# A state-space layer whose block-Toeplitz matrices are built by GpSimd's copies inside SBUF

## The chip, the core and the metric

The kernel runs on one core of a Trainium2 chip. The core has five engines that each work through their own queue of instructions in order: TensorE (PE in the profile), VectorE (DVE), ScalarE (ACT), GpSimd (POOL) and SyncE (SP). SP does nothing but start transfers. The engines wait for one another through semaphores. The metric is the device time of one execution in microseconds (us), as the median of several runs.

## The reference

One decoder layer on a sequence of 512 positions and 1024 channels, all in 32-bit floats. A normalized input `h` goes through one wide projection. Its columns feed a state-space branch (called S5), a dilated attention branch, and gates. Both branches are projected, gated, summed, projected once more and added to the input.

```
proj = h @ w_in                       -> u_s, z_s, q, k, v, z_a, r_s, r_a
S5:   h_t = A h_(t-1) + B u_t         (complex diagonal A; 64 groups, 64 states each, 16 channels each)
      y_t = Re(C h_t) + D u_t
      g   = gelu(y);  y_s = g * sigmoid(g @ w_glu);  y_s = (y_s * silu(z_s)) @ w_ssm_out
attention: 3 head groups, windows (128,1), (512,4), (2048,16), merged by softmax denominators
x + (sigmoid(r_s) * y_s + sigmoid(r_a) * y_a) @ w_o
```

The change touches the computation of `y` and of `gelu(y)`. The gelu is the tanh form, y/2 (1 + tanh(0.798 (y + 0.044715 y^3))).

## The kernel before, in words

**Projections.** Each weight tile of 128 columns is loaded by SP (`w_raw`, 512 KB), split into a high and a low part (`w_hi` on ACT, L93; `w_lo` on DVE, L95), and multiplied in three products for each of 8 row blocks: 24 matmuls of 128x512, which write a PSUM tile `pj` (L108 to L110). There are 3 such PSUM tiles, so the fourth projection from now needs the first one's tile read out by ACT. Projections that depend on nothing but `h` are used as fillers: they keep PE busy while other engines prepare the state-space branch. The last ten of them, `rs` and `ra`, are read out by a tanh on ACT (`th`, L477 and L485) and stored to HBM (`gd`, `rad`).

**The state-space branch** treats the sequence as 64 chunks of 8 positions. Its 64 groups are worked in 8 units of 8 groups, j = 0 to 7. A scan on DVE turns the inputs into the state at the end of every chunk (`Xs`). Then, for each unit:

- `ca_unit(j)` loads C (`cn`), has POOL swap its halves (L681, L682), transposes it on PE (`cps`, L685), and builds on DVE the coefficients `ab` (C times powers of A, L260 to L262). It also loads the D row (`dg`) and has POOL spread it on a diagonal (L697).
- `m_unit(j)` multiplies coefficients by B on PE (`kps`, L706), which gives the 8 impulse-response blocks K_0 to K_7 of each group. Four ACT copies bring them to the tile `kt` of 16 partitions (L710), POOL adds the D diagonal (L711). From `kt` the block-Toeplitz matrix M has to be formed: 128 partitions, where partition block t (16 partitions) holds, for each of 8 groups, the blocks shifted by t, and zeros behind them. The kernel before does it through HBM: SP stores `kt` in a buffer `kd` whose rows of 240 elements end in 112 zeros (L712), waits until it has landed, and loads M back with a source pattern of overlapping rows (L715), into one of three old buffers of the tile `dd`. The zeros are written once for all units, earlier, from a tile `zer` (L672, L673).
- `s_unit(j)` makes the shifted states for the unit, `Ss`, in the tile `uss`: POOL clears the first column of each group (L722), and ACT copies the states one column to the right, as eight copies, four large (L728) and four small (L729), because the states lie in another order than the columns.
- `y_unit(j)` computes y on PE, 32 matmuls with M and 32 with `ab` and `Ss` (`yps`, L739 and L741), read out by ACT (`ysb`, L743).
- `g_unit(j)` transposes y on PE (`yT`, L749) and applies the gelu: copy (L754) and square (L756) on ACT, a scale and add (L757) and a product (L758) on DVE, tanh on ACT (L759), a product on DVE (L760), and the split into `gT_hi` (ACT, L93) and `gT_lo` (DVE, L97).

In the written program unit j's `y_unit` stands together with `m_unit(j + 2)`, `ca_unit(j + 3)`, `s_unit(j + 1)`, `g_unit(j - 1)` and one filler. What follows the branch is the product of `gT` with `w_glu` (`pj` from `gT`), which needs all eight units of `gT` and then keeps PE busy.

**What sets the order.** The order written in Python isn't the order on the engines. A scheduler orders the instructions of each engine by a simulated time line when the program is built, and dependences become semaphore waits. So a changed edit moves instructions on every engine. Memory is shared by tags: `kt` has two buffers, so `kt` of unit j + 2 may be written only when all readers of `kt` of unit j are done; M has three; `Ss` has two.

Of the kernel before, what the change touches and what calls it, by code (L numbers as in the profile page):

```python
# [11 lines left out]
F32 = mybir.dt.float32  # L12
F32R = mybir.dt.float32r
I32 = mybir.dt.int32
AF = mybir.ActivationFunctionType
ALU = mybir.AluOpType
# [4 lines left out]
P = 128  # L21
# [6 lines left out]
Q = 16  # L28
T = 8
C = S // T  # L30
NJ = 8
NI = C // NJ
# [20 lines left out]
def tile_hybrid_block(ctx: ExitStack, tc: tile.TileContext, x, positions, norm_w, w_in, lam_re, lam_im,  # L53
# [3 lines left out]
    pe, act, dve, pool, sp = nc.tensor, nc.scalar, nc.vector, nc.gpsimd, nc.sync  # L57
# [4 lines left out]
    big = ctx.enter_context(tc.tile_pool(name="big", bufs=1))  # L62
    tmp = ctx.enter_context(tc.tile_pool(name="tmp", bufs=6))
    sml = ctx.enter_context(tc.tile_pool(name="sml", bufs=2))
    dram = ctx.enter_context(tc.tile_pool(name="dram", bufs=1, space=DRAM))
# [148 lines left out]
    for h in range(2):  # L214
# [10 lines left out]
        for q in range(KT // 2):  # L225
# [6 lines left out]
            for k in range(2):  # L232
                kk, t = 2 * q + k, slice(256 * h, 256 * h + 256)
# [3 lines left out]
                                         op0=ALU.mult, op1=ALU.subtract)  # L237
# [6 lines left out]
    Xsv = Xs.rearrange("p a i (g j) -> p a g j i", j=NJ)  # L244

    def load_u(j, Uj=None):
        if Uj is None:
            Uj = t2k("Uj")
        sp.dma_start(Uj, ud[j].rearrange("q g s c -> s q g c"))
        return Uj.rearrange("p (g c) -> p g c", g=8)  # L250
# [45 lines left out]
    for h in range(2):  # L296
        for (hi, lo), ps in first:
            for k in range(KT):
                t = slice(256 * h, 256 * h + 256)
# [77 lines left out]
    for n in (1, 2, 4):  # L377
# [3 lines left out]
        a = pw[:, :, 0:n, :]  # L381
# [285 lines left out]

    gT_hi = big.tile([P, KT, S], F32R, name="gT_hi", tag="s3")
    gT_lo = big.tile([P, KT, S], F32R, name="gT_lo", tag="s4")
    kd = dram.tile([8, Q, 8, 240], F32, name="kd")  # L670
    zer = big.tile([P, 8, 112], F32, name="zer", tag="s7b")
    pool.memset(zer, 0.0)  # L672
    sp.dma_start(kd[:, :, :, 128:240].rearrange("j q g k -> (j q) g k"), zer)  # L673

    def ca_unit(j):

# [23 lines left out]
    def m_unit(j, ca, dg):  # L700

        kt = big.tile([Q, 8, T, Q], F32, name="kt", tag=("s7a", "s7b")[j % 2])
        ps = bank("kps")
        for gg in range(8):
            a, b = gg % 4, gg // 4
            pe.matmul(ps[32 * a:32 * a + Q, b * P:(b + 1) * P], BB[:, 8 * j + gg, :], ca[:, gg, 1:9, :],  # L706
                      start=True, stop=True, skip_group_check=True, tile_position=(0, 32 * a))
        kv = kt.rearrange("q (b a) k p -> q a b (k p)", a=4)
        for a in range(4):
            act.copy(kv[:, a], ps[32 * a:32 * a + Q, 0:2 * P].rearrange("q (b m) -> q b m", b=2))  # L710
        pool.tensor_tensor(kt[:, :, T - 1, :], kt[:, :, T - 1, :], dg, op=ALU.add)  # L711
        sp.dma_start(kd[j, :, :, 0:128], kt.rearrange("q g k p -> q g (k p)"))  # L712
        M = (D1, D2, BB2)[j % 3].rearrange("p g q -> p (g q)")
        kj = kd[j]
        sp.dma_start(M.rearrange("p (g k) -> p g k", g=8),  # L715
                     bass.AP(tensor=kj.tensor, offset=kj.offset, ap=[[Q, T], [8 * 240, Q], [240, 8], [1, P]]))
        M = M.rearrange("p (g k) -> p g k", g=8)
        return M

    def s_unit(j):  # L720
        Ss = uss[:, 2 + j % 2].rearrange("p (g c) -> p g c", g=8)
        pool.memset(Ss[:, :, 0:1], 0.0)  # L722
        Sv = Ss.rearrange("p (g two) (j i) -> p two g j i", two=2, j=NJ)
        for h in range(2):
            for a in range(2):
                o = Sv[64 * a:64 * a + 64, h]
                x_ = Xsv[64 * h:64 * h + 64, a, 4 * j:4 * j + 4]
                act.copy(o[:, :, :, 1:NI], x_[:, :, :, 0:NI - 1])  # L728
                act.copy(o[:, :, 1:NJ, 0], x_[:, :, 0:NJ - 1, NI - 1])  # L729
        return Ss  # L730

    def y_unit(j, ca, M, Uj, Ss):
        ysb = t2k("ysb").rearrange("c (t m) -> c t m", t=4)
# [12 lines left out]
    def g_unit(j, ysb):  # L746
        yT = bank("yT")
        for r in range(NB):
            pe.transpose(yT[:, r * P:(r + 1) * P], ysb[:, NB - 1 - r], ident)  # L749

        yv = yT.rearrange("p (r h c) -> p r c h", h=2, r=4)
        s = t2k("gs")
        sv = s.rearrange("p (r c h) -> p r c h", r=4, h=2)
        act.copy(sv, yv)  # L754
        q = t2k("gq")
        act.activation(q, s, AF.Square)  # L756
        dve.tensor_scalar(q, q, 0.044715, 1.0, op0=ALU.mult, op1=ALU.add)  # L757
        dve.tensor_tensor(q, q, s, op=ALU.mult)  # L758
        act.activation(q, q, AF.Tanh, scale=GELU_C)  # L759
        dve.scalar_tensor_tensor(q, q, 1.0, s, op0=ALU.add, op1=ALU.mult)  # L760
        split(gT_hi[:, j], gT_lo[:, j], q, scale=0.5)
# [9 lines left out]
        for f in scan_work[i * len(scan_work) // n_scan:(i + 1) * len(scan_work) // n_scan]:  # L771
            f()

    uss = big.tile([P, 4, 512], F32, name="uss", tag="s6b")
    for j in range(2):
        Us[j] = load_u(j, uss[:, j % 2])
    Ss_[0] = s_unit(0)
    for j in range(8):
        if j + 2 < 8:
            Ms[j + 2] = m_unit(j + 2, cas[j + 2], dgs[j + 2])  # L780
        filler()
        ysbs[j] = y_unit(j, cas.pop(j), Ms.pop(j), Us.pop(j), Ss_.pop(j))
        if j + 3 < 8:
            cas[j + 3], dgs[j + 3] = ca_unit(j + 3)
        if j + 2 < 8:
            Us[j + 2] = load_u(j + 2, uss[:, j % 2])
        if j + 1 < 8:
            Ss_[j + 1] = s_unit(j + 1)
        if j > 0:
            g_unit(j - 1, ysbs.pop(j - 1))  # L790
# [363 lines left out]
```

## Time and profile before

| | |
|---|---|
| median of 3 runs | 746.56 us (746.32 to 746.74) |
| the profiled execution | 746.7 us, of which 744.9 us between first and last instruction |
| PE busy | 695.5 us (93%), 4357 matmuls |
| DVE busy | 463.3 us (62%), 914 instructions |
| ACT busy | 338.0 us (45%), 662 instructions |
| POOL busy | 170.8 us (23%), 304 instructions; it issues no transfers |
| mean granted TensorE clock | 0.975 |
| moved by DMA | 85.41 MB, 115 GB/s |

The profile counts an engine as busy while an instruction runs; issuing a transfer isn't counted. In rows of the time line the first number is the start, the second the duration, both in us, and what stands in brackets is the idle time before it and what ended it. Successive ACT, DVE and PE instructions overlap by some tens of nanoseconds to some hundreds, so a row's start-to-start distance can be less than its duration. "SPq" is the time SP takes to issue a transfer, not the transfer itself. In the text, `yps 3` is unit 3's `yps`, and likewise for the other names.

### The profile page before, as it was taken

The numbers are of one execution on the slowest core, as the hardware profiler recorded it, in microseconds if no ns is written. First come the engines' busy times: TensorE is split into PE (matmuls) and PEld (weight loads), VectorE is DVE, ScalarE is ACT, GpSimd is POOL, SyncE is SP. The second block draws the span as 40 slices with busy tenths as digits, with TensorE's granted clock in tenths as the row PEclk, the third lists the DMA queues.
The fourth block names the chain that finished last, engine by engine and source line by source line (L and its number), as shares of the span: only waits on it lengthen the run. The fifth ranks groups of instructions, "written<-read, shape, count | busy, mean of one in ns | idle before, by whom it ended". The sixth has DMA issues, their size and how long they took to land.

```text
span 744.9 us, 11696 instructions
## 1 busy us (share of the span) xinstructions
PE 695.5 (93%) x4357; PEld 573.2 (77%) x4357; DVE 463.3 (62%) x914; ACT 338.0 (45%) x662; POOL 170.8 (23%) x304
## 2 busy tenths in 40 slices
PE   2699999999989679999999999999989999999997
PEld 2687778788867467888888888878868877877886
DVE  6768756988957455575334658755764765463842
ACT  6443444334388475333144446537253733443310
POOL 3445642110011000551000315221511250230000
PEclk9899999999989889999999999999999998999999
DMA  9753644675636755455423332212312230326441
GB/s 204 128 147 105 162 110 101 120 177 147 117 103 125 137 123 149 132 165 167 141 60 114 103 96 72 85 45 71 95 48 69 71 90 28 114 71 240 157 142 56
DMA packets 153802, 85.41 MB, mean 115 GB/s; under 512 B 41097, under 2 KB 142865, under 8 KB 153617
## 3 DMA queue, kind: packets, MB, share of 16 engines
q1 hardware_dynamic: 153728, 84.66, 43.8%
q8 instruction: 34, 0.56, 0.3%
q14 instruction: 24, 0.19, 0.1%
q10 hardware_dynamic: 16, 0.00, 0.0%
HBM read 73.18 MB, written 11.47 MB: 114 GB/s over the span
## 4 chain that ended last, share of the span: by engine, by line
PE 81%; DMA 5%; ACT 4%; SPq 4%; DVE 3%; issue 1%; POOL 1%; ACTq 0%; DVEq 0%; POOLq 0%
PE pj L108 23%; PE pj L109 23%; PE pj L110 23%; PE ptp L1004 2%; PE ot L990 2%; DMA kd<-kt 1%; DMA dd<-kd 1%; DMA ral<-rad 1%; PE yps L739 1%; PE sps L934 1%; PE xps L290 1%; DMA gd<-th 1%; PE qtp L847 1%; PE yps L741 1%; PE wps L279 1%
## 5 line engine op out<-in xcount | busy, mean ns | idle before, releaser
L93 ACT ACTIVATE w_hi<-w_raw 128x1024 fp32r<-128x1024 f32 x100 | 106.0, 1061 | 239.2 <-PE pj L109 104.9
L95 DVE TENSOR_TENSOR w_lo<-w_raw,w_hi 128x1024 fp32r<-128x1024 f32 x98 | 124.8, 1274 | 106.5 <-ACT w_hi L93 105.8
L108 PE MATMUL pj<-hT_hi,w_hi 128*128 128x512 f32 (+1 forms) x344 | 134.2, 393 | 12.6 <-ACT w_hi L93 5.9
L109 PE MATMUL pj<-hT_lo,w_hi 128*128 128x512 f32 (+1 forms) x344 | 132.9, 387 | 0.7 <-DVE hT_lo L236 0.7
L110 PE MATMUL pj<-hT_hi,w_lo 128*128 128x512 f32 (+1 forms) x344 | 132.8, 387 | 0.0
L109 PE MATMUL pj<-w_lo,hT_hi 128*128 128x512 f32 (+1 forms) x288 | 106.1, 368 | 0.0
L108 PE MATMUL pj<-w_hi,hT_hi 128*128 128x512 f32 (+1 forms) x288 | 105.8, 369 | 0.0
L110 PE MATMUL pj<-w_hi,hT_lo 128*128 128x512 f32 (+1 forms) x288 | 105.1, 368 | 0.0
L108 PEld LDWEIGHTS pj<-hT_hi,w_hi 128*128 128x128 f32 x344 | 66.5, 195 | 27.5 <-ACT th L477 6.2
L109 PEld LDWEIGHTS pj<-hT_lo,w_hi 128*128 128x128 f32 x344 | 66.4, 193 | 13.7 <-DVE hT_lo L236 1.2
L110 PEld LDWEIGHTS pj<-hT_hi,w_lo 128*128 128x128 f32 x344 | 66.1, 192 | 13.7 <-DVE w_lo L95 0.3
L108 PEld LDWEIGHTS pj<-w_hi,hT_hi 128*128 128x128 f32 x288 | 54.1, 188 | 9.5 <-issue 0.2
L110 PEld LDWEIGHTS pj<-w_hi,hT_lo 128*128 128x128 f32 x288 | 54.1, 188 | 9.1
L109 PEld LDWEIGHTS pj<-w_lo,hT_hi 128*128 128x128 f32 x288 | 54.1, 188 | 8.6
L913 ACT ACTIVATE Pt<-Pt,st 128x256 f32<-128x256 f32 (+1 forms) x64 | 31.0, 491 | 18.5 <-DVE st L911 18.5
L834 POOL TENSOR_TENSOR rt<-qraw,tC 128x256 f32<-128x256 f32 x12 | 14.3, 1190 | 87.0 <-DVE qraw L828 86.7
L856 DVE SCALAR_TENSOR_TENSOR qkp<-qtp,wcol,qkp 128x512 fp32r<-128x512 f32 (+1 forms) x32 | 23.0, 746 | 13.4 <-ACT qkp L855 13.3
L943 POOL COPY sw<-st 32x4 f32<-32x4 f32 x64 | 12.0, 187 | 72.3 <-ACT Pt L913 69.5
L855 ACT ACTIVATE qkp<-qtp,wcol 128x512 fp32r<-128x512 f32 (+1 forms) x32 | 20.8, 686 | 15.6 <-PE qtp L847 10.2
L108 PE MATMUL pj<-gT_hi,w_hi 128*128 128x512 f32 x64 | 24.9, 391 | 1.4 <-ACT th L485 1.4
L262 DVE TENSOR_TENSOR ab<-ab 128x576 f32<-128x576 f32 (+1 forms) x24 | 22.0, 917 | 5.8 <-POOL ab L261 5.5
L109 PE MATMUL pj<-gT_lo,w_hi 128*128 128x512 f32 x64 | 24.9, 389 | 0.0
(275 smaller groups left out, 1336.2 us busy)
## 6 DMA issues: line engine op xcount, KB each, us to landing
w_raw<-in_w_in_dram SPq DMA_DIRECT2D x40, 512.0 KB
w_raw<-in_w_in_dram SPq DMA_DIRECT2D x112, 128.0 KB
dd<-kd SPq DMA_DIRECT2D x8, 512.0 KB
w_raw<-in_w_glu_dram SPq DMA_DIRECT2D x8, 512.0 KB
w_raw<-in_w_ssm_out_dram SPq DMA_DIRECT2D x8, 512.0 KB
w_raw<-in_w_o_dram SPq DMA_DIRECT2D x8, 512.0 KB
x_all<-in_x_dram SPq DMA_DIRECT2D x4, 512.0 KB
ud<-uT SPq DMA_DIRECT2D x8, 256.0 KB
```

Source lines behind the costliest of these rows:

```text
L93: act.activation(hi, src, AF.Copy, scale=scale)
L95: e.tensor_tensor(lo, src, hi.bitcast(F32), op=ALU.subtract)
L108: pe.matmul(o, lh, rh, start=first, stop=False, skip_group_check=True)
L109: pe.matmul(o, lh, rl, start=False, stop=False, skip_group_check=True)
L110: pe.matmul(o, ll, rh, start=False, stop=last, skip_group_check=True)
L262: dve.tensor_tensor(dst, dst, tv, op=ALU.add)
L834: pool.tensor_tensor(t1, rh[:, :, :, 0:16], cv.broadcast_to([P, NB * 2, 2, 16]), op=ALU.mult)
L855: act.activation(hi, ps[sl], AF.Copy, scale=w)
L856: dve.scalar_tensor_tensor(lo, ps[sl], w, hi.bitcast(F32), op0=ALU.mult, op1=ALU.subtract)
L913: act.activation(o, o, AF.Exp, bias=nm, scale=-1.0, accum_out=st[:, kind, 1, h, b:b + 1])
L990: pe.matmul(o, v, pts[h][:, (2 * i + k) * P:(2 * i + k + 1) * P], start=first, stop=kind == 1 and b == NB - 1 and k == 1, skip_group_check ...
L1004: pe.transpose(ps[:, (2 * i + k) * P:(2 * i + k + 1) * P], Pt[:, h, kind, 2 * bb + i, k * P:(k + 1) * P], ident)
```

## The change

Three edits.

1. **M is formed inside SBUF.** The buffer `kd`, its zero fill and the two transfers per unit on SP's queue are gone. At the start POOL clears the three M buffers once. For each unit POOL issues eight transfers, one for each partition block t: 16 partitions of `kt`, its blocks from t on, go to partitions 16t to 16t + 15 of M. The first moves 16 rows of 4 KB; the others move 128 rows of 448, 384, ... 64 bytes. Zeros behind them stay from the clearing.
2. **States in 65 columns.** `Ss` has 65 columns per group instead of 64. The first is cleared, and the 64 states of a group go to the other 64, in four ACT copies per unit instead of eight; the 65th isn't read.
3. **Gelu with one DVE operation fewer.** The factor 0.044715 goes into the square as a scale, so a tensor_scalar and a product become one scalar_tensor_tensor.

```diff
-    kd = dram.tile([8, Q, 8, 240], F32, name="kd")
-    zer = big.tile([P, 8, 112], F32, name="zer", tag="s7b")
-    pool.memset(zer, 0.0)
-    sp.dma_start(kd[:, :, :, 128:240].rearrange("j q g k -> (j q) g k"), zer)
+    Mb = [t.rearrange("p g q -> p (g q)").rearrange("p (g k) -> p g k", g=8) for t in (D1, D2, BB2)]
+    for t in (D1, D2, BB2):
+        pool.memset(t, 0.0)
...
         pool.tensor_tensor(kt[:, :, T - 1, :], kt[:, :, T - 1, :], dg, op=ALU.add)
-        sp.dma_start(kd[j, :, :, 0:128], kt.rearrange("q g k p -> q g (k p)"))
-        M = (D1, D2, BB2)[j % 3].rearrange("p g q -> p (g q)")
-        kj = kd[j]
-        sp.dma_start(M.rearrange("p (g k) -> p g k", g=8),
-                     bass.AP(tensor=kj.tensor, offset=kj.offset, ap=[[Q, T], [8 * 240, Q], [240, 8], [1, P]]))
-        M = M.rearrange("p (g k) -> p g k", g=8)
+        M = Mb[j % 3]
+        for t in range(T):
+            pool.dma_start(M[Q * t:Q * t + Q, :, 0:P - Q * t], kt[:, :, t:].rearrange("q g k p -> q g (k p)"))
         return M

     def s_unit(j):
-        Ss = uss[:, 2 + j % 2].rearrange("p (g c) -> p g c", g=8)
+        o = 1024 + 8 * (C + 1) * (j % 2)
+        Ss = uss[:, o:o + 8 * (C + 1)].rearrange("p (g c) -> p g c", g=8)
         pool.memset(Ss[:, :, 0:1], 0.0)
-        Sv = Ss.rearrange("p (g two) (j i) -> p two g j i", two=2, j=NJ)
+        Sv = Ss.rearrange("p (g two) c -> p two g c", two=2)
         for h in range(2):
             for a in range(2):
-                o = Sv[64 * a:64 * a + 64, h]
-                x_ = Xsv[64 * h:64 * h + 64, a, 4 * j:4 * j + 4]
-                act.copy(o[:, :, :, 1:NI], x_[:, :, :, 0:NI - 1])
-                act.copy(o[:, :, 1:NJ, 0], x_[:, :, 0:NJ - 1, NI - 1])
-        return Ss
+                act.copy(Sv[64 * a:64 * a + 64, h, :, 1:C + 1].rearrange("p g (j i) -> p g j i", j=NJ),
+                         Xsv[64 * h:64 * h + 64, a, 4 * j:4 * j + 4])
+        return Ss[:, :, 0:C]
...
-        act.activation(q, s, AF.Square)
-        dve.tensor_scalar(q, q, 0.044715, 1.0, op0=ALU.mult, op1=ALU.add)
-        dve.tensor_tensor(q, q, s, op=ALU.mult)
+        act.activation(q, s, AF.Square, scale=math.sqrt(0.044715))
+        dve.scalar_tensor_tensor(q, q, 1.0, s, op0=ALU.add, op1=ALU.mult)
```

The lines shift by one to four, so L725 of the changed kernel is the state copy, L709 the `kt` copy, L710 the D add, L714 the eight transfers, L721 the clearing of a column.

**POOL, around units 4 and 5, before.** POOL's queue from the D add of unit 4 to that of unit 5 (`kt_2081` is unit 4's, `kt_2212` unit 5's; `cn_2429` belongs to unit 7).

```order
L711 TENSOR_TENSOR kt_2081<-kt_2081,dg_2053 16x8x16
L722 MEMSET uss_1744 128x8
L697 TENSOR_TENSOR dg_2315<-dg_2315,ident_79 16x128
L682 COPY cn_2429<-cn_2429 128x64
L681 COPY cn_2429<-cn_2429 128x64
L711 TENSOR_TENSOR kt_2212<-kt_2212,dg_2184 16x8x16
```

The same place in the changed kernel (`kt_2091` is unit 4's, `kt_2223` unit 5's, `cn_2447` unit 7's):

```order
L710 TENSOR_TENSOR kt_2091<-kt_2091,dg_2068 16x8x16
L714 DMA dd_523<-kt_2091 16x1024
L714 DMA dd_523<-kt_2091 16x8x112
L714 DMA dd_523<-kt_2091 16x8x96
L714 DMA dd_523<-kt_2091 16x8x80
L714 DMA dd_523<-kt_2091 16x8x64
L714 DMA dd_523<-kt_2091 16x8x48
L714 DMA dd_523<-kt_2091 16x8x32
L714 DMA dd_523<-kt_2091 16x8x16
L721 MEMSET uss_1755 128x8
L696 TENSOR_TENSOR dg_2332<-dg_2332,ident_79 16x128
L681 COPY cn_2447<-cn_2447 128x64
```

The eight transfers now stand in POOL's queue between the D add and the clearing of the column for unit 4's states; the D row of unit 6 and the C tile of unit 7 come behind them. The burst of unit 5 follows in the same way, with the clearing for unit 5's states behind it, and so on to unit 7.

**ACT, around one unit's state copies, before.** Each row with what it waits for in brackets (PE_49 is PE's semaphore, DMASW those of the transfers that POOL issues).

```order
L728 COPY uss<-Xs 64x4x8x7 [waits PE_49]
L729 COPY uss<-Xs 64x4x7
L728 COPY uss<-Xs 64x4x8x7
L729 COPY uss<-Xs 64x4x7
L743 COPY ysb<-yps 128x8x4x16 [waits PE_49]
```

And in the changed kernel, from the states of unit 5 on:

```order
L725 COPY uss<-Xs 64x4x64 [waits Pool_49]
L725 COPY uss<-Xs 64x4x64
L709 COPY kt<-kps 16x2x128 [waits DMASW4_49,DMASW3_49,DMASW5_49,DMASW2_49,DMASW6_49,DMASW1_49,DMASW7_49,DMASW0_49,PE_49]
L709 COPY kt<-kps 16x2x128 x3
L725 COPY uss<-Xs 64x4x64 [waits Activation_49] x2
L740 COPY ysb<-yps 128x8x4x16 [waits PE_49]
L688 ACTIVATE p_2455<-cps 128x128 [waits DVE_49]
L751 COPY gs<-yT 128x512 [waits PE_49]
L753 ACTIVATE gq<-gs 128x512 [waits DMAHW3_49,Activation_49]
L477 ACTIVATE th<-pj 128x512
```

Before, the state copies wait for PE alone (the last reader of that buffer). Now the first of them waits for POOL's clearing of the column, which stands behind a burst in POOL's queue. And `kt` (here unit 6's) waits for all eight transfers of the unit two before it, which read the same buffer. The readout of a filler, `th`, stands behind both.

**PE, at the end of the branch, in the changed kernel.** The last transposes (`ysb_2633` is unit 6's y, `ysb_2721` unit 7's), and the first product with `gT`:

```order
L746 MATMUL yT_2756<-ident_79,ysb_2633 128x128 x4
L110 MATMUL pj_2858<-hT_hi_107,w_lo_2773 128x512
L746 MATMUL yT_2804<-ident_79,ysb_2721 128x128 x4
L108 MATMUL pj_2910<-gT_hi_1197,w_hi_2820 128x512
L109 MATMUL pj_2910<-gT_lo_1198,w_hi_2820 128x512
L110 MATMUL pj_2910<-gT_hi_1197,w_lo_2821 128x512
```

Before, 20 filler matmuls stand between these two groups of transposes and 11 between the last one and the first product with `gT`; now there are 1 and none. In both programs 168 filler matmuls stand between `yps 0` and the first product with `gT`; now they stand in front of `yps 2`, `3`, `4`, `5`, `7` and the last transposes as 28, 35, 33, 22, 49 and 1 (before 24, 30, 37 and 5 in front of `yps 2` to `5`, 41 in front of `yps 7`, then 20 and 11). `yps 6` follows `yps 5` without a filler, in both.

More of the change, by code (lines that the diff above doesn't have):

```diff
@@ L772, in tile_hybrid_block @@
             f()
-    uss = big.tile([P, 4, 512], F32, name="uss", tag="s6b")
+    uss = big.tile([P, 2 * 512 + 2 * 8 * (C + 1)], F32, name="uss", tag="s6b")
     for j in range(2):
-        Us[j] = load_u(j, uss[:, j % 2])
+        Us[j] = load_u(j, uss[:, 512 * (j % 2):512 * (j % 2) + 512])
     Ss_[0] = s_unit(0)
@@ L785, in tile_hybrid_block @@
         if j + 2 < 8:
-            Us[j + 2] = load_u(j + 2, uss[:, j % 2])
+            Us[j + 2] = load_u(j + 2, uss[:, 512 * (j % 2):512 * (j % 2) + 512])
         if j + 1 < 8:
```

## Prediction

> **What bounds the kernel now.** I first looked at stretches of time: before, in and after the stage that the change edits (from the last filler before `yps 0` to the first product with `gT`). Behind the length stand the busy times of PE, weight loads, DVE, ACT and POOL, then the granted clock, the transfers' share and GB/s.
>
> ```profile
> 110.00:206.00 96.00, 96.00 (x620) 78.10 (x619) 80.94 (x113) 36.93 (x62) 10.99 (x16) 1.00 0.59 132
> 206.00:296.00 90.00, 74.48 (x799) 59.32 (x797) 50.43 (x73) 63.48 (x140) 8.18 (x19) 0.89 0.60 126
> 296.00:420.00 124.00, 123.72 (x591) 104.10 (x592) 60.62 (x67) 42.89 (x61) 30.81 (x24) 1.00 0.43 129
> ```
>
> On both sides PE never rests, so nothing that other engines do there can be worth anything. In the 90 us between, PE is idle for 15.5 us and its granted clock falls to 0.89. POOL works 8 us of 90. PE's waits say for whom it stood (total, times, longest):
>
> ```profile
> PE pj L108 <- ACT th L477: 5.3, 2, 5.1
> PE kps L706 <- DVE ab L262: 3.3, 1, 3.3
> PE yps L741 <- ACT uss L729: 3.0, 1, 3.0
> PE yps L739 <- DMA dd<-kd: 2.5, 1, 2.5
> ```
>
> 2.5 us are put down to M's way through HBM. The chain of waits in this stretch shows it behind more than that:
>
> ```profile
> 228.88 8.11 DMA kd<-kt
> ...
> 239.58 7.01 DMA gd<-th
> ...
> 258.29 2.44 DMA kd<-kt
> 260.74 9.26 DMA dd<-kd
> ```
>
> SP's queue is in order. A store of `kt` holds the load of M, and the store of a filler's `th` behind them left at 239.58 and landed 7 us later. ACT stood for its buffer, and PE for ACT:
>
> ```profile
> 246.67 0.63 ACT L756 ACTIVATE gq<-gs 128x512 f32<-128x512 f32 x1 [4.08 <-DMA gd<-th]
> 247.84 0.80 PE L108 MATMUL pj<-hT_hi,w_hi 128*128 128x512 f32 x1 [5.08 <-ACT th L477]
> 249.29 0.63 PE L108 MATMUL pj<-hT_hi,w_hi 128*128 128x512 f32 x1
> 249.72 0.63 PE L109 MATMUL pj<-hT_lo,w_hi 128*128 128x512 f32 x1
> 253.63 0.40 PE L110 MATMUL pj<-hT_hi,w_lo 128*128 128x512 f32 x1
> 253.86 0.39 PE L108 MATMUL pj<-hT_hi,w_hi 128*128 128x512 f32 x1
> ```
>
> After such a wait PE starts slowly: matmuls 0.43 us apart instead of 0.23, 12 of them until 253, so a wait costs 2.3 us on top of itself. The most that can be had follows from PE's work at full clock:
>
> ```profile
> 284.53 0.34 PE L739 MATMUL yps<-dd,uss 128*64 128x64 f32 x4
> 286.55 0.66 PE L749 MATMUL yT<-ident,ysb 128*128 128x128 f32 x4
> 286.96 0.48 PE L110 MATMUL pj<-hT_hi,w_lo 128*128 128x512 f32 x1
> ```
>
> A unit's `yps` takes 2.0 us, a `yT` 0.4. With 168 fillers at 0.234 (39.3), eight `yps` and `yT` (19.2), and about 5 for `kps` and `cps`, the stretch needs 63.5 us of 90. So up to 26 us lie there, 3.5% of the span.
>
> **The change, cheap parts first.** Clearing M takes three POOL operations of 128x1024:
>
> ```profile
> 46.98 0.85 POOL L672 MEMSET zer<- 128x896 f32 x1 [4.86 <-DVE pw L386]
> 59.89 1.94 POOL L433 TENSOR_TENSOR ab<-dd,fT 128x1024 f32<-128x1024 f32 x1
> 64.22 2.86 POOL L261 TENSOR_TENSOR ab<-dd,AT 128x1024 f32<-128x1024 f32 x1 [2.40 <-DVE dd L435]
> ```
>
> By the first row one takes 0.97. Two stand between the other two rows, in 2.40 us of idle time; the third comes when POOL has no more coefficients to make. Cost 0; without that gap up to 2 us. The removed zero fill was hidden too.
>
> ```profile
> 209.60 0.48 PE L741 MATMUL yps<-ab,uss 128*64 128x64 f32 x4 [3.00 <-ACT uss L729]
> ...
> L728 ACT COPY uss<-Xs 64x224 f32<-64x224 f32 x31 | 18.1, 585 | 4.8 <-PE yps L741 4.4
> L729 ACT COPY uss<-Xs 64x28 f32<-64x28 f32 x32 | 7.6, 236 | 0.2
> L710 ACT COPY kt<-kps 16x256 f32<-16x256 f32 x20 | 7.2, 362 | 5.2 <-PE kps L706 4.4 <-issue 0.6
> L757 DVE TENSOR_SCALAR gq<-gq 128x512 f32<-128x512 f32 x8 | 4.2, 528 | 11.1 <-ACT gq L756 11.1
> ```
>
> State copies: 585 and 236 ns for 224 and 28 elements give 1.78 ns an element, so 256 take 640, and four follow each other in 2.2 us instead of 2.9 for eight. ACT is busy 63 of 90 us, so this counts. Against it: the large copies of unit 0 could begin before the last scan step, the new ones need it. That step ends near where PE's wait of 3.00 begins, 206.6; four copies later, `yps 0` starts near 209.0 instead of 209.6. The gelu loses 0.53 us of DVE per unit, hidden except in the last unit.
>
> **M inside SBUF.** SP's two transfers go; POOL issues eight per unit, and POOL's queue is in order too. Everything hangs on e, the time that POOL spends on one issue, which no row shows. Bounds:
>
> ```profile
> 223.60 0.61 SPq L712 DMA_DIRECT2D kd<-kt  x1
> 228.88 2.45 SPq L712 DMA_DIRECT2D kd<-kt  x1
> 257.82 0.45 POOL L711 TENSOR_TENSOR kt<-kt,dg 16x128 f32<-16x128 f32 x1 [4.70 <-ACT kt L710]
> 258.21 0.10 POOL L722 MEMSET uss<- 128x8 f32 x1
> ...
> L697 POOL TENSOR_TENSOR dg<-dg,ident 16x128 f32<-16x128 f32 x3 | 1.8, 594 | 20.6 <-DMA dg<-in_d_skip_dram 20.6
> L682 POOL COPY cn<-cn 128x64 f32<-128x64 f32 x2 | 1.6, 790 | 4.9 <-DMA cn<-in_c_re_dram 4.9
> L681 POOL COPY cn<-cn 128x64 f32<-128x64 f32 x2 | 0.5, 234 | 5.1 <-DMA cn<-in_c_im_dram 5.1
> ```
>
> SP issues the same tile's 128 rows in 0.61, which I take as the lower end; 2.45, the same with SP held up by transfers ahead, as the upper. POOL does it in software that steps through the 128 rows, and its own operation on a 16x128 tile takes 0.45. I take the sum of issue and walk, e = 1.05, since an empty queue is the nearer row. The Trainium skill (DMA: Bandwidth & Descriptors, Specifications) gives about 1 us to the first byte for GpSimd and 0.6 for SP; SP's rows agree, and with e = 1.0 the sum below would be 737.
>
> Now the new waits, from the order shown with the change. A burst (8e) stands before the clearing of the column; ACT's state copies wait for that clearing; `kt` of the next unit and the readout `th` of a filler stand behind them on ACT; and the next burst waits for `kt`. That is a loop through POOL and ACT which did not exist. I follow it with these rows and distances: four `kt` copies 1.4, `ysb`, `p`, `gs`, `gq`, `th` together 2.3 on ACT.
>
> - PE reaches `kps 3` at 215.9; `kt` and the D add make burst 3 start at 218.2. Behind it come D and C work and the next D add (0.59 + 0.79 + 0.23 + 0.45, about 2.0), so burst 4 starts at 220.2 + 8e = 228.6 and ends at 237.0.
> - ACT: state copies to 239.3, `kt 5` to 240.7, burst 5 from 241.2 to 249.6, `th` at 243.0. PE, with 28 and 35 fillers, needs that PSUM tile at 240.4: it stands 2.6.
> - Unit 6's `kt` comes after two state copies: 252.2. Burst 6 runs from 252.7 to 261.1; the next `th` is out at 255.6; PE, there at 251.9, stands 3.7.
> - 22 fillers, `kps 7`, `yps 5`: 263.9. States of unit 6 are copied by 263.4, M lands by 263.5 (2.4 for a landing, as 258.29 above): no wait. Burst 7: 265.3 to 273.7, states by 276.5; PE has 49 fillers until 277.8. `gT` starts at 280.8.
>
> ```profile
> 292.41 0.57 ACT L754 COPY gs<-yT 128x512 f32<-128x512 f32 x1
> 296.28 0.50 PE L108 MATMUL pj<-gT_hi,w_hi 128*128 128x512 f32 x1 [1.41 <-ACT th L485]
> 298.30 1.00 DVE L97 SCALAR_TENSOR_TENSOR gT_lo<-gq,gT_hi 128x512 fp32r<-128x512 f32 x1 [0.70 <-ACT gT_hi L93]
> ```
>
> The last gelu took 6.9 us from copy to `gT_lo`, hidden behind 11 fillers. No fillers cover it now. Without the removed operation it is 6.4, and PE needs its result 21 matmuls (4.9) after it begins: 1.5 of waiting. Two slow starts after the waits of 2.6 and 3.7 cost 2 each, and I allow 1.5 for one store that still lands late (SP's load of D now waits for the D add behind a burst). That makes 280.8 + 1.5 + 4 + 1.5 = 287.8 against 296.3, a gain of 8.5. The profiled execution took 746.7 (0.1 above the median of the runs): **738**.
>
> **How it depends on e.** Up to about 1.05 PE's end is set by the second `th`, 24e; beyond, all five bursts stand in line, and `gT` starts at 237.4 + 40e. At e = 0.61 the waits for `th` shrink to one of 2.5 (ACT itself), one slow start goes, and the sum gives 732. At 1.25 it gives 745, at 1.5 756, at the upper end about 794. Break-even is near 1.28.
>
> **Rivals.**
>
> - *POOL issues as fast as SP* (0.6): 732. For it: the rows are few. Against: POOL's smallest operation on that tile takes 0.45 alone.
> - *POOL's queue becomes the pace* (slower). The place: the column's clearing behind the burst. Price: 40 us per us of e; it decides from e = 1.28. At 1.5, 756. For it: POOL's rows for small work go up to 0.79 us, so one issue may well cost more than mine. Against: POOL has 82 idle us in this stretch.
> - *Hidden anyway.* The copies land late, as the load of M did (9.26 instead of 2.44). Then M of unit 6 comes at 270.4, 6.5 after PE wants it, with one more slow start: gain 0, 746.5. For it: seven of eight copies have rows under 512 bytes, and the transfers are busy to 0.60. Against: half as many bytes as before. The Trainium skill (same page and section) says that below 512 bytes the engines read, modify and write; whether that holds inside SBUF no run here shows. It also says (Issuing engines are not separate DMA queues) that another issuer saves only issue time; the chain above shows more than issue time on SP, a store that waits behind others.
>
> **Numbers.** The forecast (e from 0.8 to 1.2) has 0.44, fast issue 0.12, the POOL pace 0.34, hidden 0.10. About 0.2% (1.5 us) is what a measurement of this kernel can tell from no change. Faster: 0.42 of the first, the second, and 0.02 of the last, 0.56; same 0.08; slower 0.36. The range that leaves out two in ten goes from 731 (fast issue) to 757 (e = 1.5); the forecast's own is 733 to 745.
>
> **What would show it.** Right: POOL's queue shows eight issues of about 1 us per unit; ACT's state copies wait for POOL's clearing, 3 to 8 us for units 4 to 6; no PE wait for M but small ones; waits for `th` of 2 to 4 us; `gT` starts near 281 to 288; all after that unchanged, and nothing gained before 206. Wrong: issues above 1.3 us and a start of `gT` past 296, or PE waits for `dd` with POOL long done (late landing). If ACT never waits for POOL, the loop is my invention and the gain is larger.

## The result

The changed kernel takes 741.83 us (median of 4 runs, 739.80 to 742.48) against 746.44 us for the kernel before (4 runs, 746.19 to 746.74). The ratio is 0.9937, 95% interval 0.9920 to 0.9954: 4.6 us faster. That is inside the range of the prediction, 3.8 us above its 738. The profiled execution is the fastest of the four (739.8 us; span 737.7 instead of 744.9), so its numbers flatter the change by some 2 us.

The same three stretches of time after the change:

```profile
110.00:206.00 96.00, 96.00 (x619) 77.73 (x617) 82.38 (x114) 34.25 (x58) 24.61 (x40) 1.00 0.48 126
206.00:296.00 90.00, 76.62 (x825) 61.18 (x825) 49.38 (x65) 64.41 (x115) 32.89 (x62) 0.94 0.51 118
296.00:420.00 124.00, 124.00 (x602) 104.44 (x600) 63.66 (x72) 46.58 (x67) 27.82 (x22) 1.00 0.41 124
```

PE still never rests on either side. In the edited stretch it is busy 2.1 us more than before, at a granted clock of 0.94 instead of 0.89, and POOL works 33 us instead of 8. PE's waits from 200 to 300, and the one wait of ACT for POOL between 110 and 300 (total, times, longest):

```profile
PE pj L108 <- ACT th L477: 4.6, 2, 3.6
PE yps L738 <- ACT uss L725: 4.2, 2, 2.1
PE pj L108 <- ACT th L485: 4.1, 1, 4.1
PE kps L705 <- DVE ab L262: 0.3, 1, 0.3
...
ACT uss L725 <- POOL uss L721: 0.2, 1, 0.2
```

The wait for M is gone, and ACT hardly ever waits for POOL. But 13.2 us of waits remain where there were 15.5: the ones at `yps 0` and at the end grew. From the last filler before `yps 0` to the first product with `gT` the stage is 7.6 us shorter all the same (82.5 instead of 90.1). Most of that is pace. By its record the granted clock was 0.50 for 20.5 us in the kernel before (208.8 to 215.7, 246.4 to 253.2, 263.4 to 266.9 and 270.3 to 273.7), and for 6.8 us of the stage in the changed one (210.0 to 213.4, 257.8 to 261.2), with 3.4 more behind its end (288.5 to 291.9). At half pace 13.7 us less of that are worth up to 6.8 us, an estimate.

The groups of instructions show what an issue costs (count, total, mean in ns):

```profile
L714 POOL DMA_DIRECT2D dd<-kt x64 | 33.8, 535 | 2.4 <-POOL kt L710 2.1 <-POOL uss L721 0.2
L725 ACT COPY uss<-Xs 64x256 f32<-64x256 f32 x32 | 20.5, 640 | 0.8 <-POOL uss L721 0.2
L672 POOL MEMSET dd<- 128x1024 f32 x3 | 2.8, 953 | 0.1
```

POOL spends 0.535 us on an issue, half of what the prediction took. The view of line 714 gives the spread, and the landing of the transfers:

```profile
L714 POOL DMA_DIRECT2D dd<-kt x64: 508/531/715, 136.9 to 270.1; - x64
...
DMA to landing us min/median/max: 1.7/4.5/6.1
```

**The first product.** The time line at `yps 0`, of ACT and PE:

```profile
206.83 5.17 ACT L725 COPY uss<-Xs 64x256 f32<-64x256 f32 x8
...
208.16 0.34 PE L738 MATMUL yps<-ab,uss 128*64 128x64 f32 x4 [2.10 <-ACT uss L725]
210.74 0.48 PE L738 MATMUL yps<-ab,uss 128*64 128x64 f32 x4 [2.14 <-ACT uss L725]
211.01 0.43 PE L736 MATMUL yps<-dd,uss 128*64 128x64 f32 x4
```

ACT copies eight times in one block, two for unit 0, two for unit 1, two for unit 0, two for unit 1: so the scheduler arranged them, and all of them need the last step of the scan. `yps 0` gets going at 210.74 (before: 209.60), and its matmuls then follow at half pace until 213.4. That slow start isn't new. Before, it lasted until 215.6:

```profile
209.86 0.43 PE L739 MATMUL yps<-dd,uss 128*64 128x64 f32 x4
```

So PE comes to the last matmuls of `kps 3` at 215.99 now, and came to them at 217.26 before (there behind a `cps` and a `yT`).

**The readout in the middle.** ACT's row ahead of PE's wait of 3.60 at 256.50:

```profile
248.95 1.06 ACT L93 ACTIVATE w_hi<-w_raw 128x1024 fp32r<-128x1024 f32 x1 [0.92 <-PE pj L109]
249.91 1.31 ACT L725 COPY uss<-Xs 64x256 f32<-64x256 f32 x2
251.25 1.49 ACT L709 COPY kt<-kps 16x256 f32<-16x256 f32 x4
252.76 1.27 ACT L725 COPY uss<-Xs 64x256 f32<-64x256 f32 x2
...
255.87 0.58 ACT L477 ACTIVATE th<-pj 128x512 f32<-128x512 f32 x1
```

No step of it waits for POOL. ACT works without a break from 248.95, and the readout `th` stands at the end of its row.

**The end.** What ACT does ahead of the first product with `gT`, and that product:

```profile
286.49 0.58 ACT L485 ACTIVATE th<-pj 128x512 f32<-128x512 f32 x1
286.96 0.62 ACT L93 ACTIVATE gT_hi<-gq 128x512 fp32r<-128x512 f32 x1
287.48 0.59 ACT L485 ACTIVATE th<-pj 128x512 f32<-128x512 f32 x1
...
288.12 0.51 PE L108 MATMUL pj<-gT_hi,w_hi 128*128 128x512 f32 x1 [4.12 <-ACT th L485]
...
289.25 0.63 PE L108 MATMUL pj<-gT_hi,w_hi 128*128 128x512 f32 x1
```

The product starts 8.2 us earlier than before (296.28). But the scheduler has put nearly all fillers ahead of `yps 7`. Before, PE's order was 41 filler matmuls, `yps 7`, `yT 6`, 20 fillers, `yT 7`, 11 fillers, `gT`. Now it is 49 fillers, `yps 7`, `yT 6`, 1 filler, `yT 7`, `gT`. Two gelus and the last readouts stand uncovered on ACT. PE waits 4.12 for the last readout, not for the gelu's result, and starts at half pace.

### The profile page after: what moved, and what is told of

It is laid out like the page before. It is cut to its first block, busy times and chain, and to the rows that moved or that the text cites. A ratio compares the mean times of both kernels' runs of the same rounds, so it can differ in the third digit from the quotient of the medians.

```text
span 737.7 us, 11768 instructions
## 1 busy us (share of the span) xinstructions
PE 690.3 (94%) x4357; PEld 568.5 (77%) x4357; DVE 462.4 (63%) x906; ACT 334.6 (45%) x630; POOL 209.5 (28%) x370
## 3 DMA queue, kind: packets, MB, share of 16 engines
q0 software_dynamic: 2048, 2.36, 2.2%
## 4 chain that ended last, share of the span: by engine, by line
PE 79%; DMA 4%; ACT 4%; SPq 4%; POOL 4%; DVE 3%; issue 2%; POOLq 0%; DVEq 0%
PE pj L108 23%; PE pj L110 22%; PE pj L109 22%; PE ot L986 2%; PE ptp L1000 2%; DMA ral<-rad 1%; POOL dd L714 1%; PE sps L930 1%; PE qtp L843 1%; POOL ab L261 1%; ACT uss L725 1%; PE xps L290 1%; DMA Uj<-ud 1%; DMA w_raw<-in_w_in_dram 1%; DMA cn<-in_c_im_dram 1%
## 5 line engine op out<-in xcount | busy, mean ns | idle before, releaser
L108 PE MATMUL pj<-hT_hi,w_hi 128*128 128x512 f32 (+1 forms) x344 | 134.0, 392 | 11.4 <-ACT w_hi L93 5.4
L110 PEld LDWEIGHTS pj<-hT_hi,w_lo 128*128 128x128 f32 x344 | 66.3, 193 | 13.7 <-DVE w_lo L95 0.3
L714 POOL DMA_DIRECT2D dd<-kt x64 | 33.8, 535 | 2.4 <-POOL kt L710 2.1
L108 PE MATMUL pj<-gT_hi,w_hi 128*128 128x512 f32 x64 | 25.6, 400 | 4.1 <-ACT th L485 4.1
L851 ACT ACTIVATE qkp<-qtp,wcol 128x512 fp32r<-128x512 f32 (+1 forms) x32 | 20.8, 686 | 15.5 <-PE qtp L843 10.2
L956 POOL COPY sfb<-sd 32x2 f32<-32x2 f32 x64 | 18.2, 285 | 27.4 <-DVE sd L952 24.6
```

The costliest lines, as they stand in the source:

```text
L108: pe.matmul(o, lh, rh, start=first, stop=False, skip_group_check=True)
L110: pe.matmul(o, ll, rh, start=False, stop=last, skip_group_check=True)
L714: pool.dma_start(M[Q * t:Q * t + Q, :, 0:P - Q * t], kt[:, :, t:].rearrange("q g k p -> q g (k p)"))
L851: act.activation(hi, ps[sl], AF.Copy, scale=w)
L956: pool.tensor_copy(fb[32 * b:32 * b + 32, :, r], d[32 * r:32 * r + 32, 1, :, b])
```

## The experiments

Three theories stood at the start. **A**: M's way through HBM was the loss, its removal is worth 8 to 10 us, and the new order at the state copies and at the end gives part of that back. **B** and its kin: M's way was hidden, and the gain comes from ACT's relief or from the other order of instructions. **L**: the loop of the prediction through POOL and ACT, at a smaller price per issue.

"Stage" in the table is the distance from the start of the last filler matmul before `yps 0` to the first product with `gT`, in the profiled execution. The runs were made in three sets, each on another chip, with the kernel before measured beside them: edits 1 to 3 alone and edits 1 and 3 together, then the changed kernel again with unit 0's copies, the last filler and sixteen issues, then the rest. The times scatter more there than in the first measurement (the kernel before: 743.0 to 750.8), so the ratios to the kernel before of the same set carry the verdicts.

| kernel | median, us | ratio to before, 95% interval | stage, us |
|---|---|---|---|
| before | 745.6 to 747.0 in three sets | 1 | 90.1 |
| the changed kernel, again | 741.67 | 0.9936 (0.9910 to 0.9962) | 83.0 |
| edit 1 alone (M) | 741.21 | 0.9932 (0.9904 to 0.9961) | 79.9 |
| edit 2 alone (states) | 748.20 | 1.0015 (0.9986 to 1.0043) | 90.9 |
| edit 3 alone (gelu) | 745.85 | 0.9972 (0.9944 to 1.0000) | 89.4 |
| edits 1 and 3 | 737.46 | 0.9877 (0.9835 to 0.9920) | 78.4 |
| edit 1 in the order of before | 736.38 | 0.9876 (0.9847 to 0.9906) | 77.8 |
| changed, unit 0's copies first | 736.15 | 0.9856 (0.9814 to 0.9898) | 78.5 |
| changed, last filler behind `yps 7` | 737.56 | 0.9864 (0.9831 to 0.9897) | 80.7 |
| both mends | 730.65 | 0.9805 (0.9780 to 0.9829) | 77.9 |
| changed, copies from SP's queue | 743.14 | 0.9968 (0.9948 to 0.9989) | 86.3 |
| sixteen issues, scheduler's order | 753.84 | 1.0100 (1.0066 to 1.0134) | 93.6 |
| sixteen issues, changed kernel's order | 748.17 | 1.0040 (1.0018 to 1.0063) | 87.6 |

**Edit 1 alone.** The kernel before with `zer`, `kd` and SP's two transfers replaced by the three clearings and the eight copies of the diff above.

> Only the first edit: M by POOL's eight transfers, old state copies, old gelu. Theory A (the gain is M's way through HBM, with a POOL issue of 0.53 us as the changed kernel's profile shows, and the state copies cost about 1 us at the first yps): more than the whole gain, 738 to 741 us, first yps near 209.6 as before, gT starting near 286 to 288. Theory B (M's move is hidden or neutral, and the gain comes from a less loaded ACT and the other order of instructions): 745 to 748. In both, bursts of eight issues take 4 to 4.5 us.

Measured: 0.9932, 5 to 6 us. The median is just outside A's band, B is out. PE's waits from 200 to 300 in this kernel show what is missing:

```profile
PE kps L705 <- DVE ab L262: 4.8, 3, 3.3
PE pj L108 <- ACT th L485: 3.9, 1, 3.9
PE yps L738 <- ACT uss L726: 1.6, 1, 1.6
```

Here too the end is uncovered, 3.9.

**Edit 2 alone.** The kernel before with the 65 columns and four copies per unit.

> Only the second edit: states in 65 columns, four copies per unit, M through HBM. Theory A: the eight copies of units 0 and 1 stand in one block after the last scan step, so the first yps gets going near 210.7 instead of 209.6; behind that the waits for M and for th remain: 746 to 748 us. Theory B: ACT's relief (0.7 us per unit) shortens the waits for th: 741 to 744.

Measured: 1.0015, interval on both sides of 1, and the first `yps` gets going at 210.99, as A said. No gain, and B's 741 to 744 is excluded. Whether it costs 1 or 2 us isn't told apart from nothing.

**Edit 3 alone.**

> Only the third edit: gelu with one VectorE operation fewer. Theory A: the removed operation (0.53 us per unit) lies beside the projections except in the last unit, so within 1 us of before, 745.5 to 747. Theory B (the other order of instructions that comes with it, eight units fed a little earlier, is worth something): 742 to 745.

Measured: 0.9972, interval up to 1.0000. It may be worth a little, or nothing; undecided. Beside edit 1 it stood at 0.9877 against 0.9932 without it, and those intervals overlap as well.

**Edits 1 and 3.** The changed kernel with the old state copies.

> The changed kernel with the old state copies (edits one and three). Theory A: 1 to 3 us faster than the changed kernel, 738.5 to 741, because the first yps starts near 209.6 with warm matmuls again. Theory B (the four copies relieve ACT and pay): slower than the changed kernel, 743 to 746.

Measured: 0.9877, faster than A's band. It ran on another chip than the runs that follow. The changed kernel was run once more, as their base:

> The changed kernel once more, as the base of the three runs beside it. Theory A (M's move alone is worth 8 to 10 us, and the state copies give part of it back): again 4 to 7 us under the kernel before. Theory C (the difference between the changed kernel and the one without the state edit is only that they ran on different chips): 8 to 10 us under the kernel before, like that one.

0.9936, as in the first measurement: C is out. The state edit gives back some 4 us beside the others, though the two intervals overlap a little.

**Edit 1 in the order of before.** Every change so far also let the scheduler reorder the other engines. Here each engine's issue order is held as it was before, by order edges without waits:

```
+    for e, runs in ORDER.items():              # order of the kernel before, engine by engine
+        seq = []                               # the instructions at these places
...
+        for x, y in zip(seq, seq[1:]):
+            tc.add_manual_dep(y, x.name, no_sync, reason="held order")
```

> Only the first edit, with the issue order of every engine held as it was before: POOL's eight transfers stand right behind each D add, the two transfers of M on SP's queue are left out, nothing else moves. Theory P (the path itself is worth the time: no wait for M of 2.5, no store that holds up a readout of 5.1, fewer slow starts, and the eleven fillers that cover the last gelu stay): 6 to 10 us under the kernel before, more than the 5.8 that the same edit gave in the scheduler's own order. Rival (the path was hidden and the gain came with the new order): within 2 us of the kernel before.

Measured: 0.9876, 9.2 us, inside P's band. The path itself is worth the time; the rival is out. PE's waits from 200 to 300 in this kernel:

```profile
PE kps L705 <- DVE ab L262: 4.6, 3, 3.3
PE yps L738 <- ACT uss L726: 1.6, 1, 1.6
PE pj L108 <- ACT th L485: 1.4, 1, 1.4
PE pj L108 <- ACT th L477: 1.3, 2, 1.0
PE yps L736 <- DMA cn<-in_c_re_dram: 0.7, 1, 0.7
```

The waits for M (2.5) and for the readout behind a late store (5.1) are gone, one of 3.3 for DVE's coefficients has stayed, and the end is covered by 11 fillers as it was: 1.4 instead of 3.9. One wait of 0.7 at a product with M is put down to the load of `cn`. `gT`'s product starts at 284.67, 77.8 us after the last filler (before: 90.1), though the waits fell only from 15.5 to 9.7: the granted clock was 0.50 for 3.4 us instead of 20.5. The scheduler's own order for the same edit took some 4 us of the gain (0.9932 against 0.9876; the two were measured on different chips, and their intervals just touch).

**Unit 0's copies first.** The changed kernel with

```
+        if j == 0:
+            copies(0, NI - 1)          # needs all but the last scan step
+            copies(NI - 1, NI)
+        elif j == 1:
+            with tc.issue_after(s0_last[0].ins):   # behind unit 0's on ACT
+                copies(0, NI)
...
```

> The changed kernel, but unit 0's state copies in two steps (four of 64x224 before the last scan step, four of 64x32 behind it), and unit 1's copies queued behind them on ACT. Theory A: the first yps starts near 208 instead of 208.2 and 210.7 in two pieces, and with warm matmuls; 2 to 3 us faster than the changed kernel. Rival (the state copies' place is not what costs; the changed order of the instructions behind does): within 1 us of the changed kernel.

Measured: 5.5 us under the changed kernel of the same set, twice what A said. In PE's time line of this kernel `yps 0` starts early and at full pace:

```profile
207.44 0.34 PE L753 MATMUL yps<-ab,uss 128*64 128x64 f32 x4 [1.36 <-ACT uss L732]
207.60 0.29 PE L751 MATMUL yps<-dd,uss 128*64 128x64 f32 x4
```

The wait there falls from 4.2 to 1.4, and there is no half pace right behind it. The waits for `th` L477 fall from 4.6 to 2.4, in an order that changed from unit 1 on. How much belongs to the copies and how much to that order wasn't separated.

**Last filler behind `yps 7`.**

```
+    with tc.issue_after(last_y[0].ins):   # last_y: the last matmul of yps 7
+        while fill:                       # one filler is left, 24 matmuls
+            filler()
     g_unit(7, ysbs.pop(7))
```

> The changed kernel with one thing moved: the 24 matmuls of the last filler are queued behind yps 7 instead of ahead of it; nothing else on PE moves. Theory A (the 4.1 us wait for the last readout before gT's product is a gelu chain that nothing covers): the wait is gone and with it the slow start of 0.7, 4 to 5 us faster than the changed kernel. Rival (the wait only moves: yps 7 is reached 5.4 us sooner, near 275, and the burst of unit 7 ended at 270.7 with landings of up to 6.1): up to 1.5 us of wait for M of unit 7 and a slow start of 2, so a gain of 1 us or none.

Measured: 4.1 us under the changed kernel, as A said. The product with `gT` runs at full pace (25.0, 24.9 and 24.9 us in its three lines instead of 25.6, 25.6 and 25.5), and PE's waits from 200 to 300 in this kernel show 1.4 ahead of it:

```profile
PE pj L108 <- ACT th L477: 4.6, 2, 3.6
PE yps L740 <- ACT uss L725: 4.5, 3, 2.1
PE pj L108 <- ACT gs L754: 1.4, 1, 1.4
```

**Both mends.**

> The changed kernel with both mends: unit 0's state copies in two steps with unit 1's behind them, and the last filler's 24 matmuls queued behind yps 7. Theory A (two separate losses): 5.5 and 4.1 add up, 9 to 10 us faster than the changed kernel, 731 to 733. Rival (what one mend gains, the other loses: yps 7 is reached some 8 us sooner and waits for M of unit 7 or for its states): 735 to 737, like one mend alone.

Measured: 730.65 (4 runs), ratio 0.9805: in the time the two mends add up. This version beats the kernel before by 14.9 us in the medians of one set, and the changed kernel by 11.0 in those of two sets, 9.8 by the ratios. Its stretch in the view of windows:

```profile
206.00:296.00 90.00, 80.64 (x852) 64.06 (x851) 51.27 (x68) 65.37 (x118) 33.63 (x62) 0.98 0.54 122
```

PE is busy 4.0 us more in these 90 us than in the changed kernel, at a granted clock of 0.98. What the rival named is there too, at a smaller price: `yps 7` is reached sooner, waits for its states, and then runs at half pace.

```profile
272.92 0.34 PE L755 MATMUL yps<-ab,uss 128*64 128x64 f32 x4 [1.86 <-ACT uss L732]
...
274.06 0.43 PE L753 MATMUL yps<-dd,uss 128*64 128x64 f32 x4
```

So the stage is 5.1 us shorter than the changed kernel's (77.9 against 83.0), less than the 4.5 and 2.3 of the two mends by themselves. Part of the rest lies behind the stage, where the product with `gT` begins at full pace.

**Sixteen issues.** Each copy cut in two halves of four groups:

```
         for t in range(T):
-            pool.dma_start(M[Q * t:Q * t + Q, :, 0:P - Q * t], kt[:, :, t:]...)
+            for b in range(0, 8, 4):
+                pool.dma_start(M[Q * t:Q * t + Q, b:b + 4, 0:P - Q * t], kt[:, b:b + 4, t:]...)
```

> The changed kernel with every one of the eight transfers cut in two halves of four groups: sixteen issues per unit, the same bytes. A burst then takes about 8.5 us, what the prediction assumed for eight. Theory L (the prediction's loop through POOL and ACT is there, but at 0.53 per issue has slack): the state copies of units 4 to 6 now wait for POOL's clearing 2 to 6 us each, and the time grows by 5 to 8 us. Rival (POOL's queue has room; nothing waits for it): within 2 us of the changed kernel.

Measured: 12 us slower than the changed kernel, more than either theory said. But the reason isn't L's. The scheduler gave this kernel another order: it cleared the columns ahead of the bursts, and ACT waited for POOL 0.2 us in all. What PE waited for was the readouts, which in this order stand behind ACT's copies; of its waits from 200 to 300 the largest is:

```profile
PE pj L108 <- ACT th L477: 12.2, 4, 4.2
```

So this run tests the scheduler more than the loop. Held in the changed kernel's order, the same sixteen issues do test it:

> The changed kernel with sixteen issues of half the size per unit, and the issue order of every engine held as in the changed kernel, so that the clearing of a column stands behind a burst of about 8.3 us instead of 4.2. Theory L (the prediction's loop through POOL and ACT, with slack at eight issues): ACT's state copies wait for POOL's clearing, 2 to 4 us in each of the units 4 to 7; 6 to 12 us slower than the changed kernel. Rival (the 12 us of the sixteen issues before came from the order that the scheduler chose for them, with readouts late behind ACT's copies, and no engine waits for POOL): within 3 us of the changed kernel.

Measured: 748.17, 6.5 us above the changed kernel by the medians, 7.8 by the ratios. Now the loop closes. The time line of this kernel: POOL's burst of unit 4 with the clearing behind it, and ACT's state copies of units 4 to 7:

```profile
231.26 4.59 POOL L715 DMA_DIRECT2D dd<-kt  x9 [0.29 <-POOL kt L710]
236.27 0.51 POOL L715 DMA_DIRECT2D dd<-kt  x1 [0.42 <-DMA dd<-kt]
...
240.44 0.13 POOL L723 MEMSET uss<- 128x8 f32 x1
...
240.60 2.66 ACT L727 COPY uss<-Xs 64x256 f32<-64x256 f32 x4 [4.34 <-POOL uss L723]
...
255.49 1.29 ACT L727 COPY uss<-Xs 64x256 f32<-64x256 f32 x2 [1.53 <-POOL uss L723]
...
267.37 2.65 ACT L727 COPY uss<-Xs 64x256 f32<-64x256 f32 x4 [2.41 <-POOL uss L723]
...
281.72 1.32 ACT L727 COPY uss<-Xs 64x256 f32<-64x256 f32 x2 [3.14 <-POOL uss L723]
```

11.4 us of waits in four pieces, and PE's waits for `th` L477 grow from 4.6 to 9.5 us. L holds. The bursts of units 4 to 7 last 9.2, 9.8, 8.1 and 9.2 us here, since POOL in three of them also waits between issues for transfers that have not landed; in the changed kernel it never did.

**Copies from SP's queue.** `pool.dma_start` of the eight copies becomes `sp.dma_start`.

> The changed kernel with the eight copies inside SBUF issued from SP's queue instead of POOL's. Theory Q (the way through HBM was the loss; which queue issues the copies hardly matters, since they take about as long to issue): within 2 us of the changed kernel. Rival (SP's queue is in order, and the copies stand behind weight loads and stores that hold it up, as the load of M did before): M lands late, PE waits for dd, 4 us or more slower than the changed kernel.

Measured: 0.9968, some 2.4 us behind the changed kernel, with intervals that overlap: between the two theories, undecided. SP spends 0.60 us on an issue (median, against POOL's 0.53). M isn't late: the only wait of PE at a product with M is 0.2 us, and no transfer ended it, while those for `th` L477 are 6.1 instead of 4.6. The Trainium skill (DMA: Bandwidth & Descriptors, Issuing engines are not separate DMA queues), which the prediction weighed, says that another issuing engine saves only the time of issuing. This run doesn't speak against it: with either queue PE no longer waits for M.

## Why the prediction was right, and where it was wrong

The time and the sign were right, and the mechanisms too. The terms were off in both directions and cancelled. The forecast's sum had the first product with `gT` start at 287.8; the profile shows 288.12. That they agree so well is luck:

| us | forecast | measured |
|---|---|---|
| PE at the last part of `kps 3` | 215.9 | 216.0 |
| waits for `th` | 6.3 | 4.6 |
| slow starts | 4 | 1.7 (estimate: half of 3.4) |
| a store that lands late | 1.5 | 0 |
| wait at the end | 1.5 | 4.1 |
| PE's own work from `kps 3` to `gT` | 58.6 (280.8 - 215.9 - 6.3) | 61.7 (estimate: 288.1 - 216.0, less 8.7 of waits and 1.7) |

- **Where the time can come from** held. Nothing was gained before 206 but half a microsecond (the last filler starts at 205.67 instead of 206.20), and nothing behind the start of `gT` (449.6 us to the end instead of 448.6).
- **M's way through HBM was the loss**: shown by the run that changes the path alone. "Hidden anyway" is out: no kernel with POOL's copies waited more than 1.4 us in one place for M, and the changed one didn't wait at all. Its transfers land in at most 6.1 us; in other kernels with POOL's copies up to 8.9.
- **e was mis-sized**: 1.05 forecast, 0.535 measured, below even the lower bound of 0.61. That bound was SP's issue of one transfer with 128 rows; nothing made it a bound for POOL. And "issue and walk" don't add: an issue takes 0.51 to 0.72 us whether it has 16 long rows or 128 short ones. The about 1 us to the first byte that the Trainium skill (DMA: Bandwidth & Descriptors, Specifications) gives for GpSimd is not the price of an issue here. SP's 0.61, in which the prediction saw agreement, is the time of an issue too, and no row here shows the time to a first byte. The step made the forecast too pessimistic: its own sum gave 732 at 0.61.
- **The loop** was right as a mechanism, and idle in the changed kernel. The prediction said that ACT's copies would wait 3 to 8 us in units 4 to 6; at the measured e they waited 0.2. With bursts of about 9 us they waited 1.5 to 4.3. The price was about right too: the forecast's slope between 0.61 and 1.05 is 13.6 us per us of e, which for 5 us more per burst gives 8.5; measured 6.5 to 7.8. What it said for the case that ACT never waits (the loop an invention, the gain larger) was wrong on both counts.
- **The start of `yps 0`** failed. The step took four copies of 640 ns (measured 640) in 2.2 us behind the last scan step, hence 209.0. Four in a row take 2.65, so a unit's copies save ACT 0.3 us and not 0.7. And the step did not read in what order ACT's copies of units 0 and 1 stand: they alternate, so `yps 0` waits for all but the last two of the eight, until 210.74. In this profile that cost nothing against the forecast, which was met at `kps 3`: the half pace behind `yps 0` lasted 3.4 us, and 6.8 in the kernel before. But the time can be had: the mend of this step is worth 5.5 us, part of it through the order behind it.
- **The end** failed. "1.5 of waiting" assumed one gelu between `yps 7` and `gT`, and that PE would wait for its result. There were two on ACT, with the readouts of the last fillers between and behind them, and PE waited 4.1 for the last readout. Another 1.6 went by the slow start of the product, whose 192 matmuls begin within 45.0 us instead of 43.4 before. The mend is worth 4.1.
- **PE's own work** was too small. The stage, less its waits and half of its time at half pace, is about 66 us in the changed kernel (82.5 - 13.2 - 3.4), in edit 1 in the order of before (77.8 - 9.7 - 1.7) and 67 with both mends (77.9 - 9.2 - 1.7), all estimates; the prediction counted 63.5. Where the rest lies stays open.
- **The waits for `th`**: 2.6 and 3.7 forecast, 1.0 and 3.6 measured. The first was forecast at 240.4 and stood at 224.5, in front of `yps 2`. The second has the right size for the wrong reason: not a burst of POOL, but ACT's unbroken row from 248.95.
- **Slow starts**: two were charged at 2 us, behind the waits for `th`. There was one there, behind the wait of 3.60, and one each at `yps 0` and at `gT`.
- **Clearing M, the gelu, late stores**: the clearings are hidden as forecast (953 ns each, the first two at 62.04 in the gap named). The gelu is at most a small gain. The 1.5 us for a late store was not needed.

With e as measured, the forecast's sum is at or below the 732 that it gave at 0.61, where `gT` would have started near 282.0. The changed kernel is some 10 us above that: about 6 by the start of `gT` (the end, PE's own work, the waits for `th`), 1 behind it, and 2 because the profiled execution was the fastest. The two mends bring 9.8 back by the ratios (0.9936 to 0.9805), to 730.65, but not the same 9.8: PE's own work hasn't changed.

Of the rivals, "as fast as SP" had the price of an issue nearly right and the time wrong, by the end, PE's own work and the waits for `th`. "POOL's queue paces" is real, and here closer than its break-even of 1.28: bursts of 8.1 to 9.8 us, about 1.15 per issue of the original eight, are already 0.4% slower than before, with the uncovered end and PE's own work in the time. (The line 237.4 + 40e itself gives 754.8 at 1.5 and break-even near 1.30, not 756 and 1.28.)

## What to carry to other kernels

Where a scheduler orders the instructions, an edit's own price and the price of the order that comes with it are two numbers: hold the order fixed to measure the first, then look in the new order for work that lost its cover (the last fillers, the first copies). An edit that shortens the wait for one input can be worth half its price until the fillers are placed again. And before a loop between engines is priced by a guess of an issue, ask how much slack it has at half that guess.

## What was not expected of the hardware

- POOL's issue of a transfer inside SBUF took 508 to 715 ns (64 issues, median 531), and 512 ns (median) for copies of half the size. The median is 532 ns for the eight with 16 rows and 531 for all: in these sizes the cost is per issue, not per row or byte.
- Whether PE's half pace comes behind a wait isn't told by the wait's length. Behind waits of 2.36 us (both mends) and 3.27 us (sixteen issues, held order) the next matmuls stood 0.23 us apart; behind 1.86 (both mends, at `yps 7`), 2.41 (unit 0's copies first), 3.00 (before, at `yps 0`), 3.60 and 4.12 us (the changed kernel) they stood at half pace at once or soon. The row behind the 2.41:

```profile
251.97 0.50 PE L108 MATMUL pj<-hT_hi,w_hi 128*128 128x512 f32 x1 [2.41 <-ACT th L477]
...
253.47 0.63 PE L108 MATMUL pj<-hT_hi,w_hi 128*128 128x512 f32 x1
253.90 0.63 PE L109 MATMUL pj<-hT_lo,w_hi 128*128 128x512 f32 x1
```

  In the record of the granted clock the stretches at 0.50 between 200 and 300 us last 3.41 us or twice that in every kernel of the table, and in one execution they begin whole multiples of 3.41 apart (changed kernel: 210.03, 257.81 and 288.53, which are 14 and 9 times 3.41). The waits of 2.10 and 2.14 at `yps 0` were followed by one such stretch in the first profile of the changed kernel and by two in the second. The Trainium skill (TensorE: Matmul & The Clock Gate, Part 1: The HAM clock gate) puts the window at about 3.4 us, free-running; the record agrees with that. So the 2 us that the prediction added to a wait of 2.6 could have come or not.
- A small wait early in the kernel can cost more than twice its length. In the repeat of the changed kernel PE waited 1.87 us for the load of `Uj`, up to 98.05, and its time line shows half pace behind it (0.43 us apart), until 105:

```profile
98.05 1.40 PE L290 MATMUL xps<-Uj,W 128*64 128x64 f32 x20 [1.87 <-DMA Uj<-ud]
102.67 0.63 PE L108 MATMUL pj<-hT_hi,w_hi 128*128 128x512 f32 x1
103.10 0.63 PE L109 MATMUL pj<-hT_lo,w_hi 128*128 128x512 f32 x1
```

  Its last filler before `yps 0` started at 210.69 instead of 205.67, while the stage itself took as long as in the first profile (83.0 and 82.5). Edits are better compared by the length of their stage than by one execution's time.
